# A streaming encoder layer on one core: the heads' mean squares and the samples' attention in column tiles of the array

## The chip, the cores and the metric

The kernel runs on one core of a Trainium2 chip. The metric is the device time of one execution in microseconds, from several runs of the same program; lower is better. The core has a matrix engine (PE, with its weight loads as PEld), a vector engine (DVE), a scalar engine (ACT), a general engine (POOL) and an engine that issues transfers (SP). Each takes its own instructions in a queue, and they wait for each other by semaphores.

## The reference

The reference is one layer of an encoder with two branches, for a prompt of 1024 frames and for 32 further frames of a running stream (here: the samples), which sees 512 cached frames. Width is 1024, all in fp32. One input projection gives the queries, keys and values of a gated linear attention (4 heads) and of a differential attention (8 heads of two 64-wide halves), and gates. What the change touches is the second branch:

```
def diff_attend(q, k, v, mask, lam):
    s = einsum('bqhmd,bkhmd->bhmqk', q, k) * (DIFF_HD ** -0.5)
    if mask is not None: s = where(mask, s, -inf)
    p = softmax(s, axis=-1)
    attn = p[:, :, 0] - lam * p[:, :, 1]
    return einsum('bhqk,bkhe->bqhe', attn, v)
...
yd = rmsnorm(o_diff, diff_subln_g) * (1 - lambda_init) * silu(dg)
merged = sigmoid(ma) * (yg @ w_proj_gla) + sigmoid(mb) * (yd @ w_proj_diff)
return x + rmsnorm(merged @ w_out, post_norm_g)
```

So each head has two score matrices, two softmaxes and one output of 128 channels for each frame, and that output is divided by the root of its mean square over the 128 channels.

## The kernel before

The work runs in stages: input norm and values (to about 270 us), the gated branch (to about 600 us), the differential branch (to about 1177 us), the projection of the gated branch (pg), the projection of the differential one (pd), and the output matrix with the last norm. Most matmuls run in a split form of three products (high times high, low times high, high times low), 352 or fewer columns each; these are the ps_w rows of lines 464 to 466, 486 to 488 and 1122 to 1124.

In the differential stage three threads share PE, and a planner (class `Order`, lines 62 to 123) writes out PE's order by hand while the program is built. A thread is a generator. It yields, ahead of a group of PE instructions, the group's cost in us, the events it needs with a latency each (table `W`, line 52), and the PSUM banks it takes; the planner keeps a clock, takes the first thread in its list that is ready, and adds the cost. The clock is the planner's own: nothing is measured. Only PE's order is fixed this way, the other engines' is left to the framework. The threads, first choice first:

- `diff_main` (line 923), the prompt's heads one after another. `diff_scores` (892) makes a 128-row tile of scores (ps_s, lines 906 and 907) and its softmax on DVE and ACT; the tile is transposed (ps_t, 954) and multiplied with the values (po, 967 to 969). Output `osb` and its square `sqo` (970, 971) hold a head transposed, channels on the 128 partitions and 1024 frames along them. `diff_fin` (878) then forms the mean square of each frame, which is a sum over partitions and so a matmul with `one_h`, a 128x128 matrix of 1/128: two steps of 512 frames into a bank `o` (ps_m, 882). All 128 result rows are equal; ACT copies row 0 back into `sqo` (883), and SP stores the 1024 numbers as row h of `msd` (885). Then DVE multiplies `osb` by the gate (888) and SP stores it (889). The steps of head h run just behind the first score tile of head h + 1. `sqo` has one buffer. `msd` is read once, behind the stage (1154), for all heads' roots; the roots come back as `rsb` and scale the loaded `ydr` (1164).
- `sample_thread` (977), the 32 samples, two heads at a time. Their keys are loaded from the cache (`load_k`), then the scores come: head and half m lie in rows ((h - h0) * 2 + m) * 32 of one bank, so four tiles of 64 rows x 32 columns of the array are used (ps_ss, lines 1009 and 1011, at `tile_position=(m * HD, r0)`; 512 cached and 32 own keys). Each head is a step of its own, with its value load (`load_v`) issued behind it on SP; the values take the place of the keys in SBUF. Softmax, transposes (ps_st, 1029), and the outputs: each head is a step that takes the bank `o`, four 128-row matmuls over the cached values and one 32-row matmul over the own ones, all in one strip of 32 columns (po_s, 1041 and 1042), and one ACT copy (1043). Norm and a transpose (ps_so, 1052) end the pair.
- `fill` (469), projections of the input for later heads and for the gates, in pieces of two k-steps (ps_w, 486 to 488). It runs where the others are not ready. The stage ends when the last head's output and the last of these jobs are done.

In this stage there are two banks for ps_w (`pj`), two double ones for scores (`s`), one for transposes (`t`) and one for outputs (`o`). An fp32 matmul that is not split is run by PE as two passes, each with its own weight load.

Of the kernel before, what the change touches and what calls it, by code (L numbers as in the profile page):

```python
# [14 lines left out]
AF = mybir.ActivationFunctionType  # L15
# [5 lines left out]
P = 128  # L21
NP = 1024
NS = 32
# [3 lines left out]
PAST = 512  # L27
GH, GDV = 4, 256
DH, HD = 8, 64
# [97 lines left out]
def hybrid_step_kernel(ctx: ExitStack, tc: tile.TileContext, a):  # L127
    nc = tc.nc
    mm = nc.tensor.matmul
    act = nc.scalar.activation  # L130
    ve = nc.vector
    dma = nc.sync.dma_start
    st = nc.sync.dma_start
# [26 lines left out]
    def dbank(name):  # L160
        return bank_of("s", name)
# [4 lines left out]
    def obank(name):  # L166
        return bank_of("o", name)
# [16 lines left out]
    one_h = cst.tile([P, P], F32, name="one_h")  # L184
# [691 lines left out]
        return BLK_DG + h, ("dg", h), begin, [(("fin", h - 1), 0.0)] if h else []  # L876

    def diff_fin(h, osb, sqo):
        for n0 in (0, 512):
            yield 0.86, [(("pv", h, 3), W["pv"])], ["o"]  # L880
            ps = obank("ps_m")
            mm(ps, one_h, sqo[:, n0 : n0 + 512], start=True, stop=True)
            act(sqo[0:1, n0 : n0 + 512], ps[0:1], AF.Copy)
            S.free("o", W["m_o"])
        st(msd[h : h + 1, :], sqo[0:1, :])
# [91 lines left out]
    def sample_thread():  # L977
# [11 lines left out]
        def load_v(h):  # L989
            vcs = ctile(h, [P, 4, P], "vcs")  # L990
            dma(vcs, a["cachev"][:, h * P : h * P + P].rearrange("(c p) e -> p c e", p=P))
            dma(vsm[0:NS, h % 2], a["newv"][NP:T, h * P : h * P + P])
            S.mark(("sv", h))
            return vcs

        for h0 in range(0, DH, 2):
            hs = (h0, h0 + 1)
            kcs = [load_k(h) for h in hs]
            vcs = []
            for h, kc in zip(hs, kcs):  # L1000
                if h == h0:
                    yield 0.6, [(("dk", h0 + 1), W["sdk"]), (("dg", h0 + 1), W["sdg"]), (("kc", h), W["kc"])], ["s"]
                    ps = dbank("ps_ss")
                else:
                    yield 0.6, [(("kc", h), W["kc"])], []
                for m in range(2):
                    r0 = ((h - h0) * 2 + m) * 32
                    hr = slice(m * HD, m * HD + HD)
                    mm(ps[r0 : r0 + 32, 0:PAST], qsam[h][hr, :], kc[hr, :], start=True, stop=True,
                       tile_position=(m * HD, r0))  # L1010
                    mm(ps[r0 : r0 + 32, PAST:w], qsam[h][hr, :], ksam[h][hr, :], start=True, stop=True,
                       tile_position=(m * HD, r0))
# [20 lines left out]
                S.free("t", W["st_t"])  # L1033
            S.mark(("spt", h0))
            os_ = tp.tile([64, P], F32, tag="yt", name="os_")
            for h in hs:
                yield 0.6, [(("spt", h0), W["spt"]), (("sv", h), W["sv"])], ["o"]
                r = slice((h - h0) * 32, (h - h0) * 32 + 32)
                o = obank("po_s")[r, 0:P]
                for c in range(4):  # L1040
                    mm(o, pT[:, c, h - h0, :], vcs[h - h0][:, c, :], start=(c == 0), stop=False, tile_position=(0, r.start))
                mm(o, pT[0:NS, 4, h - h0, :], vsm[0:NS, h - h0], start=False, stop=True, tile_position=(0, r.start))
                act(os_[r], o, AF.Copy)
# [281 lines left out]
```

## Time and profile before

| | us |
|---|---|
| median of 3 runs | 1478.51 |
| lowest, highest | 1473.87, 1479.91 |
| the profiled execution | 1477.82 |
| its span, first to last instruction | 1476.1 |
| mean granted clock of PE | 0.99 |
| ps_m, po_s, ps_ss groups (PE busy, 600 to 1177 us) | 14.4, 11.7, 6.7 |
| PE busy in that stage's ps_w (L486 to L488) | 754.2 |

The page gives, for each engine, busy time and its share of the span. Matmuls overlap each other in PE, so their printed durations add up to more than the time they fill (the last row of the table is longer than the stage); the distance from one start to the next is what a matmul takes of PE. A row of the timeline holds start, duration, engine, line, operation, what is written from what, the part of the array as rows*columns, the shape, and the count of merged instructions. A row of the chain of waits says who waited for whom: us in total, times, longest us.

### The profile page before, as it was taken

To read this page: it belongs to the slowest core of one execution; us is meant where nothing else is said; L and a number is where in the kernel's file an instruction comes from. 1 tells how busy PE (TensorE), PEld (TensorE's weight loads), DVE (VectorE), ACT (ScalarE), POOL (GpSimd) and SP (SyncE) were. 2 spreads that over 40 slices of the span, in tenths; PEclk is the share of its full clock that TensorE was granted. 3 is DMA by queue.
4 is the path that set the end of the run, shared out by engine and by line. 5 is a ranking of instruction groups with operands and counts; after the bars stand their busy time and mean duration, and the time that the engine had idled before them with its cause. 6 is when DMAs were issued, how large, how long until landed. Compare 5 with 4: busy or idle time off the path is not lost.

```text
span 1476.1 us, 22367 instructions
## 1 busy us (share of the span) xinstructions
PE 1422.4 (96%) x8848; PEld 1327.5 (90%) x8848; DVE 789.9 (54%) x1464; ACT 600.5 (41%) x1262; POOL 300.2 (20%) x186
## 2 busy tenths in 40 slices
PE   8999999989999999899999999999899899999997
PEld 6787779889999899899989998998899799999997
DVE  5602005756565343576776766678665536455415
ACT  4513114535354233455555555555455432221311
POOL 1200002222223124223222222222221111122001
PEclk9999999999999999999999999999999999999999
DMA  8620111122222233313232332223222278634205
GB/s 303 211 107 31 45 50 50 54 73 73 87 64 86 71 109 110 98 54 116 68 100 69 97 90 93 75 77 90 92 69 80 96 265 306 222 132 132 101 1 193
DMA packets 66742, 156.58 MB, mean 106 GB/s; under 512 B 10008, under 2 KB 28568, under 8 KB 65600
## 3 DMA queue, kind: packets, MB, share of 16 engines
q1 hardware_dynamic: 66624, 155.01, 32.5%
q8 instruction: 74, 1.21, 0.4%
q14 instruction: 44, 0.36, 0.1%
HBM read 104.39 MB, written 40.04 MB: 98 GB/s over the span
## 4 chain that ended last, share of the span: by engine, by line
PE 51%; DVE 6%; DMA 4%; ACT 2%; issue 1%; POOL 1%; SPq 0%; DVEq 0%; POOLq 0%; ACTq 0%
PE ps_w L486 9%; PE ps_w L487 9%; PE ps_w L488 9%; PE ps_w L465 2%; PE ps_w L464 2%; PE ps_w L466 2%; PE ps_s L907 2%; PE ps_t L954 2%; PE ps_s L906 2%; PE ps_c L1216 2%; PE ps_c L1218 2%; PE ps_c L1217 2%; DMA ydr<-ydd 1%; DMA kl<-kl 1%; PE po L968 1%
## 5 line engine op out<-in xcount | busy, mean ns | idle before, releaser
L486 PE MATMUL ps_w<-X,wh 128*128 128x352 f32 x1344 | 452.5, 337 | 1.4 <-DVE vo L292 1.1
L487 PE MATMUL ps_w<-X,wl 128*128 128x352 f32 x1344 | 437.7, 326 | 0.0
L488 PE MATMUL ps_w<-X,wh 128*128 128x352 f32 x1344 | 435.7, 324 | 0.0
L456 POOL TENSOR_TENSOR wl<-wr,wh 128x1024 fp32r<-128x1024 f32 x72 | 180.5, 2507 | 656.3 <-ACT wh L454 493.1
L486 PEld LDWEIGHTS ps_w<-X,wh 128*128 128x128 f32 x1344 | 255.0, 190 | 5.5 <-issue 3.0
L487 PEld LDWEIGHTS ps_w<-X,wl 128*128 128x128 f32 x1344 | 255.4, 190 | 1.2 <-issue 1.2
L488 PEld LDWEIGHTS ps_w<-X,wh 128*128 128x128 f32 x1344 | 254.7, 190 | 0.0
L912 ACT ACTIVATE p<-ps_s,nm 128x256 f32<-128x256 f32 (+7 forms) x128 | 94.6, 741 | 58.8 <-DVE ps_s L908 30.8
L306 PE MATMUL ps_v<-wh,X 128*128 128x512 f32 x248 | 97.6, 394 | 1.2 <-DVE X L245 1.2
L305 PE MATMUL ps_v<-wh,X 128*128 128x512 f32 x248 | 98.5, 397 | 0.2 <-DVE g L343 0.2
L307 PE MATMUL ps_v<-wl,X 128*128 128x512 f32 x248 | 98.3, 396 | 0.0
L454 ACT ACTIVATE wh<-wr 128x1024 fp32r<-128x1024 f32 x72 | 75.9, 1054 | 54.6 <-PE ps_w L488 30.6
L910 DVE TENSOR_REDUCE nm<-ps_s 128x1 f32<-128x256 f32 (+7 forms) x128 | 94.8, 747 | 2.7
L292 DVE TENSOR_TENSOR vo<-ps_v,vo 32x512 f32<-32x512 f32 x4 | 2.7, 678 | 140.8 <-ACT vo L291 140.8
L908 DVE MEMSET ps_s<- 64x64 f32 x128 | 14.3, 112 | 115.9 <-PE ps_s L907 114.3
L671 POOL TENSOR_TENSOR vl<-vr,vh 128x512 fp32r<-128x512 f32 (+1 forms) x20 | 24.6, 1228 | 219.4 <-ACT vh L670 219.4
L906 PE MATMUL ps_s<-k,q 128*128 128x512 f32 (+2 forms) x192 | 68.0, 362 | 1.2 <-DMA k<-k 1.2
L907 PE MATMUL ps_s<-kl,q 128*128 128x512 f32 (+2 forms) x192 | 63.8, 348 | 3.7 <-DMA kl<-kl 3.7
L288 ACT ACTIVATE vo<-ps_v 128x512 f32<-128x512 f32 x32 | 19.1, 595 | 115.1 <-PE ps_v L307 114.7
L956 ACT ACTIVATE ah<-ps_t 128x512 fp32r<-128x512 f32 (+2 forms) x96 | 46.9, 488 | 43.5 <-PE ps_t L954 42.7
L957 DVE TENSOR_TENSOR al<-ps_t,ah 128x512 fp32r<-128x512 f32 (+2 forms) x96 | 53.2, 554 | 18.3 <-ACT ah L956 17.0
L465 PE MATMUL ps_w<-Y,wl 128*128 128x352 f32 x192 | 62.2, 324 | 0.0
(319 smaller groups left out, 2968.8 us busy)
## 6 DMA issues: line engine op xcount, KB each, us to landing
wr<-w SPq DMA_DIRECT2D x72, 512.0 KB
thd<-gate SPq DMA_DIRECT2D x16, 528.0 KB
xn<-xn SPq DMA_DIRECT2D x16, 512.0 KB
wr<-wv SPq DMA_DIRECT2D x16, 512.0 KB
newk<-rr SPq DMA_DIRECT2D x8, 528.0 KB
ygr<-ygd SPq DMA_DIRECT2D x8, 528.0 KB
tha<-thd SPq DMA_DIRECT2D x8, 528.0 KB
ydr<-ydd SPq DMA_DIRECT2D x8, 528.0 KB
```

The lines of the kernel that those rows point to most:

```text
L305: mm(ps, xk[:, 0, t0 : t0 + P], wh[:, k, :], start=(k == 0), stop=False)
L306: mm(ps, xk[:, 1, t0 : t0 + P], wh[:, k, :], start=False, stop=False)
L307: mm(ps, xk[:, 0, t0 : t0 + P], wl[:, k, :], start=False, stop=(k == KT - 1))
L456: nc.gpsimd.tensor_tensor(wl, wr, wh.bitcast(F32), op=ALU.subtract)
L465: mm(ps[:, :n], wl[:, k, :], src[k][:, 0, t0 : t0 + n], start=False, stop=False)
L486: mm(ps[:, :n], wh[:, k, :], src[k][:, 0, t0 : t0 + n], start=(k == 0), stop=False)
L487: mm(ps[:, :n], wl[:, k, :], src[k][:, 0, t0 : t0 + n], start=False, stop=False)
L488: mm(ps[:, :n], wh[:, k, :], src[k][:, 1, t0 : t0 + n], start=False, stop=(k == KT - 1))
L906: mm(ps[:, n0 : n0 + n], qs[m][:, qsl], ks[m][:, n0 : n0 + n], start=True, stop=False)
L907: mm(ps[:, n0 : n0 + n], qs[m][:, qsl], kls[m][:, n0 : n0 + n], start=False, stop=True)
L910: ve.tensor_reduce(nm, ps[:, 0:w], axis=AX.X, op=ALU.max, negate=True)
L912: act(p[:, 0:w], ps[:, 0:w], AF.Exp, bias=nm, accum_out=sm[:, m : m + 1])
```

## The change

Three edits. `diff_fin` has one step in place of two. The 1024 frames of `sqo` are taken as four runs of 256, each multiplied with 32 columns of `one_h` into its own 32 partitions of one bank, at column positions 0, 32, 64 and 96 of the array; ACT copies the 128x256 block back, and the store takes one row out of each 32 as a quarter of `msd[h]`. The step's cost in the plan is 0.5 (it was 0.86 twice).

```
-        for n0 in (0, 512):
-            yield 0.86, [(("pv", h, 3), W["pv"])], ["o"]
-            ps = obank("ps_m")
-            mm(ps, one_h, sqo[:, n0 : n0 + 512], start=True, stop=True)
-            act(sqo[0:1, n0 : n0 + 512], ps[0:1], AF.Copy)
-            S.free("o", W["m_o"])
-        st(msd[h : h + 1, :], sqo[0:1, :])
+        yield 0.5, [(("pv", h, 3), W["pv"])], ["o"]
+        ps = obank("ps_m")[:, 0:256]
+        for n in range(4):
+            mm(ps[32 * n : 32 * n + 32], one_h[:, 0:32], sqo[:, n * 256 : n * 256 + 256], start=True, stop=True,
+               tile_position=(0, 32 * n))
+        act(sqo[:, 0:256], ps, AF.Copy)
+        S.free("o", W["m_o"])
+        st(msd[h].rearrange("(n t) -> n t", n=4), sqo[0:P:32, 0:256])
```

The samples' scores of both heads of a pair are one step (cost 1.1, was 0.6 twice), which needs both heads' cached keys; first the four matmuls over cached keys, then the four over own keys, and the value loads of both heads behind them.

```
-            vcs = []
-            for h, kc in zip(hs, kcs):
-                if h == h0:
-                    yield 0.6, [(("dk", h0 + 1), W["sdk"]), (("dg", h0 + 1), W["sdg"]), (("kc", h), W["kc"])], ["s"]
-                    ps = dbank("ps_ss")
-                else:
-                    yield 0.6, [(("kc", h), W["kc"])], []
-                for m in range(2):
...
-                vcs.append(load_v(h))
+            yield 1.1, [(("dk", h0 + 1), W["sdk"]), (("dg", h0 + 1), W["sdg"])] + [(("kc", h), W["kc"]) for h in hs], ["s"]
+            ps = dbank("ps_ss")
+            for cached in (True, False):
+                for h, kc in zip(hs, kcs):
+                    for m in range(2):
+                        r0 = ((h - h0) * 2 + m) * 32
+                        hr = slice(m * HD, m * HD + HD)
+                        k, c = (kc, slice(0, PAST)) if cached else (ksam[h], slice(PAST, w))
+                        mm(ps[r0 : r0 + 32, c], qsam[h][hr, :], k[hr, :], start=True, stop=True,
+                           tile_position=(m * HD, r0))
+            vcs = [load_v(h) for h in hs]
```

The samples' outputs of both heads are one step (cost 0.8, was 0.6 twice), which needs both heads' values; the heads alternate, head n in the strip of columns 32n, and one ACT copy takes both.

```
-            for h in hs:
-                yield 0.6, [(("spt", h0), W["spt"]), (("sv", h), W["sv"])], ["o"]
...
-                act(os_[r], o, AF.Copy)
-                S.free("o", W["so_o"])
+            yield 0.8, [(("spt", h0), W["spt"])] + [(("sv", h), W["sv"]) for h in hs], ["o"]
+            o = obank("po_s")[:, 0:P]
+            for c in range(5):
+                for n in range(2):
+                    kw, v = (P, vcs[n][:, c, :]) if c < 4 else (NS, vsm[0:NS, n])
+                    mm(o[32 * n : 32 * n + 32], pT[0:kw, c, n, :], v, start=(c == 0), stop=(c == 4),
+                       tile_position=(0, 32 * n))
+            act(os_, o[0:64], AF.Copy)
+            S.free("o", W["so_o"])
```

More of the change, by code (lines that the diff above doesn't have):

```diff
@@ L998, in sample_thread @@
             kcs = [load_k(h) for h in hs]
-            vcs = []
-            for h, kc in zip(hs, kcs):
-                if h == h0:
-                    yield 0.6, [(("dk", h0 + 1), W["sdk"]), (("dg", h0 + 1), W["sdg"]), (("kc", h), W["kc"])], ["s"]
-                    ps = dbank("ps_ss")
-                else:
-                    yield 0.6, [(("kc", h), W["kc"])], []
-                for m in range(2):
[L1007 to L1012, printed above, removed]
-                vcs.append(load_v(h))
+            yield 1.1, [(("dk", h0 + 1), W["sdk"]), (("dg", h0 + 1), W["sdg"])] + [(("kc", h), W["kc"]) for h in hs], ["s"]
[9 more added lines that the diff above has]
+            vcs = [load_v(h) for h in hs]
             nm = tp.tile([P, 1], F32, tag="nm", name="nm")
@@ L1035, in sample_thread @@
             os_ = tp.tile([64, P], F32, tag="yt", name="os_")
-            for h in hs:
-                yield 0.6, [(("spt", h0), W["spt"]), (("sv", h), W["sv"])], ["o"]
[L1038 to L1043, printed above, removed]
-                S.free("o", W["so_o"])
+            yield 0.8, [(("spt", h0), W["spt"])] + [(("sv", h), W["sv"]) for h in hs], ["o"]
[7 more added lines that the diff above has]
+            S.free("o", W["so_o"])
             ss = tp.tile([64, 1], F32, tag="ss", name="ss")
```

## The prediction

> **What bounds the kernel now.** I read the page's engine line first, then the busy time by stretches and the list of who waited for whom, then the timeline of PE around each operation that the diff touches, and the chain of waits for the places where PE is not the one that is late.
>
> ```profile
> PE 1422.4 (96%) x8848; PEld 1327.5 (90%) x8848; DVE 789.9 (54%) x1464; ACT 600.5 (41%) x1262; POOL 300.2 (20%) x186
> ```
>
> PE is busy for 96% of the span. A share over the whole span says nothing of one stage, so here are three stretches, two inside the differential-attention stage (about 600 to 1177 us, where all of the edits lie) and one just behind it:
>
> ```profile
> core 0: us, PE busy (x) PEld busy (x) DVE busy (x) ACT busy (x) POOL busy (x), PEclk, DMA share, GB/s
> 700.00:800.00 100.00, 96.79 (x628) 90.32 (x627) 69.66 (x135) 51.89 (x119) 23.37 (x11) 1.00 0.27 77
> ...
> 1000.00:1100.00 100.00, 93.97 (x601) 87.76 (x600) 72.57 (x135) 51.11 (x120) 24.37 (x12) 0.98 0.27 80
> ...
> 1200.00:1260.00 60.00, 59.39 (x366) 58.51 (x366) 29.81 (x31) 17.68 (x16) 14.48 (x6) 1.00 0.83 301
> ```
>
> In both stretches of the stage PE is busy 94 to 97 us of 100, at a full clock, while DVE has 27 us free and ACT 48. What PE waits for, from 600 to 1177 us:
>
> ```profile
> PE ps_t L954 <- DVE al L957: 4.1, 3, 1.4
> PE ps_st L1029 <- DVE smp L1032: 3.6, 2, 2.3
> PE ps_t L954 <- DVE smp L1055: 1.7, 1, 1.7
> PE ps_so L1052 <- DVE al L957: 1.2, 2, 0.7
> PE ps_s L907 <- DMA kl<-kl: 1.0, 2, 0.5
> PE ps_t L954 <- DVE ps_s L908: 0.9, 3, 0.3
> PE po L967 <- ACT os__13014 L1043: 0.4, 1, 0.4
> PE ps_t L954 <- DVE p L917: 0.3, 1, 0.3
> ```
>
> Together 13.2 us of 577. The planner puts a projection matmul (ps_w) into nearly every gap, so a slot of PE that is freed is taken by the next step. In this stage a microsecond less on PE is a microsecond less in the stage, up to where the projections run out. So I price the edits in PE slots: from the start of one matmul to the start of the next, since the printed durations overlap.
>
> **Heads' mean squares (L880 to L885).** Before, each head has two steps, each one 128x512 fp32 matmul that runs as two passes:
>
> ```profile
> 671.73 0.32 PE L488 MATMUL ps_w<-X,wh 128*128 128x352 f32 x1
> 671.89 1.02 PE L882 MATMUL ps_m<-sqo,one_h 128*128 128x512 f32 x2
> 672.35 0.73 PE L486 MATMUL ps_w<-X,wh 128*128 128x352 f32 x1
> 672.92 0.32 PE L487 MATMUL ps_w<-X,wl 128*128 128x352 f32 x1
> ```
>
> A ps_w slot is 0.16 us (671.73 to 671.89). From 671.89 to 672.92 is 1.03; less one ps_w slot, the pair takes 0.87 us, 0.435 a pass of 512 columns. How often:
>
> ```profile
> L882 PE MATMUL ps_m<-sqo,one_h 128*128 128x512 f32 x28 | 14.4, 595 | 0.0
> L1041 PE MATMUL po_s<-vcs,smp 128*32 128x128 f32 x64 | 8.5, 276 | 0.0
> ```
>
> 28 passes up to 1177 us are the 14 matmuls of heads 0 to 6: 14 x 0.87 = 12.2 us. (Head 7's two come later.)
>
> After, a head has one step of four matmuls of 256 columns, each in its own strip of 32 columns of the array. The trace holds this kind of work in the samples' scores, which already use four tiles (64 rows x 32 columns):
>
> ```profile
> 730.02 0.32 PE L488 MATMUL ps_w<-X,wh 128*128 128x352 f32 x1
> 730.26 1.08 PE L1009 MATMUL ps_ss<-kc,smp 64*32 64x512 f32 x8
> 731.15 0.26 PE L1011 MATMUL ps_ss<-smp 64*32 64x32 f32 x8
> 731.34 0.43 PE L486 MATMUL ps_w<-X,wh 128*128 128x352 f32 x1
> 731.60 0.32 PE L487 MATMUL ps_w<-X,wl 128*128 128x352 f32 x1
> ```
>
> Eight passes of 512 columns take 0.89 us (730.26 to 731.15); one after another they would take 8 x 0.435 = 3.5. So four run at a time, two rounds. The timeline cut at 730.35 us shows the first round alone, four passes begun within 0.09 us:
>
> ```profile
> 730.26 0.65 PE L1009 MATMUL ps_ss<-kc,smp 64*32 64x512 f32 x4
> ```
>
> The same rows price the change to tiles and back. In: 730.02 to 730.26, less the 0.16 slot, 0.08. Out: L486 to L487 is 0.26 in place of 0.16, 0.10. And 731.15 to 731.34 is 0.19 for two rounds of 32 columns, which by the pass above are 0.03 each: 0.13 of stagger and draining. A new step is thus 2 rounds x 0.435/2 + 0.13 + 0.18 = 0.74 us, and seven take 5.2: **7.0 us saved**. What no row shows is four streams through all 128 rows; in the scores each half of the rows carries two. Bounds: four at once 0.74, two at once 1.18, none at once 2.05. I take 0.74, since the one row with four tiles shows four.
>
> On ACT one copy of 128x256 replaces two of 1x512; ACT has 48 us free in 100 and no row of the waits above names this copy, so nothing. If it did name it, the bank would still come back once a head and not twice, which is a gain. The store of the result now has four rows of 1 KB where it had one of 4 KB; its issue was:
>
> ```profile
> L885 SPq DMA_DIRECT2D msd<-sqo x8: 235/245/253, 676.4 to 1189.6; - x8
> ```
>
> SP waits in order, and what is queued behind this store are the weight loads; they wait for the copy once, as before. Between nothing and one such issue more a head, 8 x 0.25 = 2 us, all on SP; PE's list above shows no wait for a weight load, so I take nothing. Head 7's step falls into the projection stage, where PE waits for its data anyway (last fence of this part): between 0 and 1.0 us, I take 0.
>
> **Samples' outputs (L1036 to L1044).** Before, each head has its own step: 8 passes of 128 columns (64 in all = 8 heads) and two on 32 rows:
>
> ```profile
> 748.16 1.06 PE L1041 MATMUL po_s<-vcs,smp 128*32 128x128 f32 x8
> 749.15 0.40 PE L1042 MATMUL po_s<-smp 32*32 32x128 f32 x2
> 749.48 0.43 PE L486 MATMUL ps_w<-X,wh 128*128 128x352 f32 x1
> ```
>
> 1.32 us inside, and 0.18 into tiles and out: 1.50 us, 8 times, 12.0 us. These passes use one strip of 32 columns and follow each other at 1.32/10. After, the two heads of a pair alternate in two strips. If strips run beside each other as in the scores, the pair's step is as long as one head's: 4 x 1.50 = 6.0, **6.0 us saved**. The bounds are that and no overlap, 4 x (2 x 1.32 + 0.18) = 11.3, 0.7 saved. I take the first. For the last pair the second step lay on the chain itself, with the bank's copy behind it:
>
> ```profile
> 1172.57 1.06 PE L1041 MATMUL po_s<-vcs,smp 128*32 128x128 f32 x8
> ...
> 1174.32 0.39 PE L967 MATMUL po<-ah,vh 128*128 128x256 f32 x1 [0.36 <-ACT os__13014 L1043]
> ...
> 1186.67 0.43 PE L1124 MATMUL ps_w<-y,wh 128*128 128x352 f32 x1 [0.51 <-DVE y L1093]
> ```
>
> So there the saving holds although the projections have run out: 1.75 us from 1172.57 to 1174.32 go. (The last row is PE waiting for data around head 7's mean square.) The merged step waits for both heads' value loads and for the bank at once; behind it on PE stand the ps_w and ps_s matmuls. No row of the waits names a value load, so I price this at nothing.
>
> **Samples' scores (L1000 to L1013).** The order inside a tile stays cached keys, then own keys; only the order between tiles changes. At 730 us the planner had already put both heads next to each other, and all 16 passes took 1.07 us. A gain is left only where it had not, and of the four pairs that is one; its second head came by itself, four passes of 512 columns and not eight:
>
> ```profile
> 877.27 1.06 PE L1009 MATMUL ps_ss<-kc,smp 64*32 64x512 f32 x4
> 878.15 0.23 PE L1011 MATMUL ps_ss<-smp 64*32 64x32 f32 x4
> 878.32 0.43 PE L486 MATMUL ps_w<-X,wh 128*128 128x352 f32 x1
> ```
>
> The second half's 1.05 us and its 0.18 of changes go: **1.2 us saved**. The value loads, which were issued between the heads, now come behind both; that is at most 1.1 us later on SP, and the values are used at 748.16, 17 us behind the scores. Hidden by that stretch; without it 4 x 1.1 us.
>
> **Sum.** 7.0 + 6.0 + 1.2 = 14.2 us. The profiled execution took 1477.82 us around a span of 1476.1, 0.7 below the median of the runs. 1477.8 - 14.2 = 1463.6 us.
>
> **Rivals.** (a) PE starts matmuls strictly in their order. Then a mean square's second pass, queued behind its first in the same strip, holds up the next strip: five rounds in place of two, 3 x 0.218 = 0.65 us a head, and in the outputs 11 rounds for 10, 0.1 a pair. The saving is 14.2 - 7 x 0.65 - 0.4 = 9.2 us, 1468.6. In the code the own keys of each tile stand ahead of the next tile's cached keys, yet all eight L1009 passes began ahead of the first L1011; that speaks against it, if PE's queue has the code's order. The Trainium skill (TensorE: Matmul & The Clock Gate, Part 3, what overlaps and what doesn't) does say that matmuls start and end in program order; by that rule the time would be the 1468.6 of this rival, and the trace does not bear the rule out. The rival has 7%. Its neighbour, two strips at a time, saves 7 x 0.44 = 3.1 us less, 1466.7; 7%.
>
> (b) Strips of full height do not overlap at all: mean squares 7 x (2.05 - 1.74) = 2.2 us longer, outputs 0.7 and scores 1.2 shorter: 1478.1. The scores' row speaks against it. 3%.
>
> (c) The gain is lost behind the stage. There PE is 99% busy but the DMA engines are too, with 83% (1200 to 1260), and they bring the next projection its ydr (L1089). These loads stand behind head 7's own steps and so move with them; but if the queues move less than PE does, half of the gain goes, 1470.7. 10%, half of it on either side of that.
>
> (d) The changed costs move every step of the plan, and the 13.2 us of waits are drawn anew. A few us either way lie in the forecast; 4 to 8 us more give 1468 to 1472. 12%.
>
> (e) Slower: less PE work between heads lets PE reach a head's first scores before its keys' copies have landed:
>
> ```profile
> 1102.32 6.11 DMA kl<-kl
> ```
>
> Now that costs 1.0 us in all. If seven heads waited 2.0 us each, the gain would be gone; at 3.1 us each, 21.7 in all, it is 7.5 us slower, and at the whole 6.1 it would be 1506. Against it: the planner's clock now charges 0.5 and 0.8 us for steps that I put at 0.74 and 1.50, so it allows the copies more real time, not less. 5%.
>
> **Numbers.** My forecast, 1463.6 give or take the waits, has 56%. 0.5% of the time is 7.4 us, about what a measurement of this kernel can tell from no change; faster means below 1471. The forecast, (a) with its neighbour, three quarters of (d) and half of (c) lie there: 56 + 14 + 9 + 5, 0.84. Same are (b) and the rest of (c) and (d): 0.11. Slower is (e): 0.05. The range runs from 1458, where head 7's 1.0 us and some 4.5 us of waits go too, to 1471, which takes in (a) and most of (d) and leaves out 16 in 100 above.
>
> **What would show it.** Right: four L882-like matmuls of 128*32, 128x256, starting within 0.1 us of each other, their slot near 0.74; po_s in four groups of 1.3 us; one group of 16 score passes in every pair; the last po matmul about 14 us earlier than 1177, and the last instruction by the same. Wrong: the four strips in a staircase (a); rows of PE waiting for kl or smp that add up to over 20 us in the stage (d, e); the stage 14 us shorter but the end not (c).

## The result, and the profile after

| us | before | after |
|---|---|---|
| median | 1477.95 (6 runs, 1473.87 to 1480.96) | 1487.78 (6 runs, 1486.10 to 1491.33) |
| profiled execution, its span | 1477.82, 1476.1 | 1490.72, 1488.9 |
| mean granted clock of PE | 0.99 | 0.982 |

The ratio is 1.0073, with a 95% interval of 1.0057 to 1.0088: slower, by 9.8 us. The forecast was 1463.6 us, so it misses by 24.2 us, and in the sign.

The engine line of the page after:

```profile
PE 1415.8 (95%) x8880; PEld 1325.6 (89%) x8880; DVE 807.0 (54%) x1464; ACT 591.1 (40%) x1250; POOL 299.8 (20%) x186
```

PE has less work (1422.4 before) in a span that is 12.8 us longer. So the instructions did not become dearer; PE stands idle, or runs slow. The groups themselves, from PE's timeline after: the heads' mean squares, the samples' outputs, and the samples' scores.

```profile
670.75 0.32 PE L488 MATMUL ps_w<-X,wh 128*128 128x352 f32 x1
671.00 0.64 PE L883 MATMUL ps_m<-sqo,one_h 128*32 128x256 f32 x8
671.57 0.43 PE L486 MATMUL ps_w<-X,wh 128*128 128x352 f32 x1
671.83 0.32 PE L487 MATMUL ps_w<-X,wl 128*128 128x352 f32 x1
...
728.56 1.06 PE L1010 MATMUL ps_ss<-kc,smp 64*32 64x512 f32 x8
729.44 0.24 PE L1010 MATMUL ps_ss<-smp 64*32 64x32 f32 x8
729.61 0.43 PE L486 MATMUL ps_w<-X,wh 128*128 128x352 f32 x1
...
746.55 1.07 PE L1041 MATMUL po_s<-vcs,smp 128*32 128x128 f32 x16
747.54 0.41 PE L1041 MATMUL po_s<-smp 32*32 32x128 f32 x4
747.88 0.38 PE L908 MATMUL ps_s<-k,q 128*128 128x256 f32 x1
```

Eight passes of a mean square take 0.57 us (671.00 to 671.57), plus 0.09 in (670.75 to 671.00, less a slot of 0.16) and 0.10 out: 0.76 us, where 0.74 was forecast. Sixteen score passes of both heads take 1.05 us, and the twenty output passes of both heads 1.33 us, as long as one head's before. Cut at 671.05 us, the timeline shows the four strips at once:

```profile
671.00 0.42 PE L883 MATMUL ps_m<-sqo,one_h 128*32 128x256 f32 x4
```

The stretches that answer to those of before:

```profile
700.00:800.00 100.00, 96.10 (x646) 91.13 (x645) 74.49 (x139) 51.82 (x118) 24.37 (x11) 1.00 0.26 74
...
1000.00:1100.00 100.00, 94.55 (x623) 88.84 (x622) 75.25 (x141) 51.66 (x123) 24.23 (x11) 0.98 0.29 82
...
1160.00:1200.00 40.00, 30.16 (x170) 25.78 (x169) 17.71 (x25) 15.00 (x26) 2.97 (x2) 0.79 0.46 156
1200.00:1260.00 60.00, 54.21 (x324) 53.34 (x323) 24.81 (x26) 16.59 (x15) 11.40 (x5) 0.97 0.76 260
```

By busy share the middle of the stage looks as before. What differs by it is the end, where PE has 30.16 us of 40 at a clock of 0.79 (before: 35.27 at 0.96), and the next stage (54.21 of 60, before 59.39). What PE waits for from 600 us to the stage's last matmul at 1183.9:

```profile
PE ps_st L1028 <- DVE smp L1031: 8.7, 4, 2.6
PE ps_t L956 <- DVE al L959: 8.6, 8, 1.6
PE ps_t L956 <- DVE ps_s L910: 5.8, 4, 2.5
PE ps_st L1028 <- DVE al L959: 2.1, 1, 2.1
PE ps_so L1052 <- DVE al L959: 1.4, 1, 1.4
```

26.6 us, against 13.2 before. None of it is for a transfer of keys; all of it is for DVE, by a transpose (ps_t, ps_st, ps_so) whose bank or operand DVE has not finished. One such place, PE first, then DVE and POOL in the same 4 us:

```profile
741.17 0.64 PE L883 MATMUL ps_m<-sqo,one_h 128*32 128x256 f32 x8
744.42 0.27 PE L1028 MATMUL ps_st<-ident,p 128*32 128x128 f32 x1 [2.61 <-DVE smp L1031]
```

```profile
740.43 2.37 POOL L938 TENSOR_TENSOR vl<-vr,vh 128x1024 fp32r<-128x1024 f32 x1 [9.79 <-ACT vh L937]
740.93 2.95 DVE L890 SCALAR_TENSOR_TENSOR osb<-osb,gs_half,sg 128x1024 f32<-128x1024 f32 x1 [0.38 <-ACT osb L973]
743.80 0.15 DVE L917 RECIPROCAL sm<-sm 128x2 f32<-128x2 f32 x1
743.88 0.40 DVE L1031 TENSOR_TENSOR smp<-ps_st,smp 128x256 f32<-128x256 f32 x1
```

PE's next instruction behind the mean square is the samples' last transpose, whose bank is freed by DVE's add (L1031, 743.88). On DVE that add stands behind the gate multiply of the head (L890), which takes 2.95 us. PE had no projection piece in between. It came so in heads 1, 3 and 5. Before, the same wait (ps_st, smp) made 3.6 us in two places.

To add all this up, PE's timeline of each kernel was cut into parts: the stage from its first score matmul to its last projection matmul (L486 to L488), in that part every gap above 0.45 us beyond the matmul's own slot ("waits"), half of the time at half clock ("clock"), and the rest ("work"); then the tail to the last po matmul; then the time from there to the first matmul of the pd stage. From pd to the end it is 196.1 us in both. (A gap is the distance from one start to the next, less the slot. The first 12 us of the stage are left in the work: there PE waits 3.3 us for `kl` in every one of the kernels below, and its clock is at half for 6.8 us, in e18 for 3.4.)

| us | start of the stage | work | waits | clock | tail | to pd | span |
|---|---|---|---|---|---|---|---|
| before | 595.7 | 557.5 | 13.2 | 1.7 | 8.9 | 102.9 | 1476.1 |
| after | 595.2 | 544.2 | 22.0 | 5.1 | 17.3 | 108.9 | 1488.9 |

The work fell by 13.3 us, nearly what was forecast. It was given back twice over, in four places: waits 8.8, clock 3.4, tail 8.4, next stage 6.0.

The tail, in the timeline of PE and in stretches of 4 us:

```profile
1166.55 0.32 PE L488 MATMUL ps_w<-X,wh 128*128 128x352 f32 x1
1166.71 0.49 PE L956 MATMUL ps_t<-ident,p 128*128 128x128 f32 x3
1169.34 0.66 PE L1028 MATMUL ps_st<-ident,p 128*128 128x128 f32 x4 [2.15 <-DVE al L959]
...
1176.30 1.11 PE L956 MATMUL ps_t<-ident,p 128*128 128x128 f32 x4 [1.50 <-DVE al L959]
...
1179.50 0.41 PE L970 MATMUL po<-al,vh 128*128 128x256 f32 x1
1179.71 0.41 PE L971 MATMUL po<-ah,vl 128*128 128x256 f32 x1
```

```profile
1172.00:1176.00 4.00, 2.79 (x20) 1.54 (x16) 0.78 (x3) 1.27 (x4) 0.54 (x1) 0.50 0.36 123
1176.00:1180.00 4.00, 2.29 (x9) 1.77 (x10) 1.34 (x4) 0.60 (x1) 0.00 (x0) 0.50 0.00 0
1180.00:1184.00 4.00, 4.00 (x22) 4.00 (x21) 0.00 (x0) 0.00 (x0) 0.00 (x0) 0.55 0.66 206
```

The projections run out at 1166.55 while the last head's transposes, a whole pair of samples' transposes and outputs and the last po are still to come. Before, the samples' transposes began at 1166.85, while projections still ran (to 1168.10), and half of the outputs came right behind. After, each wait is bare, and behind the waits PE is granted half its clock: four transposes take 0.66 us at 1169.34 and 1.11 at 1176.30. In the built order, 343 of the 380 projection pieces (six matmuls each) that lie behind the stage's first score matmul stand ahead of the mean square of head 6; before, it was 340. So three pieces fewer were left for the end.

In the next stage PE waits for the gated branch's evacuation (`tha`, the step that takes the sums out of PSUM) on DVE, from 1184 us on after and from 1177 us on before:

```profile
PE ps_w L486 <- DVE tha L1105: 5.7, 4, 2.7
```

```profile
PE ps_w L486 <- DVE tha L1105: 0.8, 2, 0.5
```

That evacuation stands behind DVE's scaling of ydr (L1164). After, DVE sits idle in front of that scaling for 13.7 us, waiting for the loads of ydr and rsb, before for 6.0.

### The profile page after: what moved, and what is told of

It is laid out like the page before. It is cut to its first block, busy times and chain, and to the rows that moved or that the text cites. A ratio compares the mean times of both kernels' runs of the same rounds, so it can differ in the third digit from the quotient of the medians.

```text
span 1488.9 us, 22417 instructions
## 1 busy us (share of the span) xinstructions
PE 1415.8 (95%) x8880; PEld 1325.6 (89%) x8880; DVE 807.0 (54%) x1464; ACT 591.1 (40%) x1250; POOL 299.8 (20%) x186
## 4 chain that ended last, share of the span: by engine, by line
PE 46%; DVE 11%; ACT 4%; DMA 3%; issue 2%; POOL 1%; SPq 0%; DVEq 0%; POOLq 0%; ACTq 0%
PE ps_w L486 8%; PE ps_w L487 8%; PE ps_w L488 8%; PE ps_w L465 2%; PE ps_w L464 2%; PE ps_w L466 2%; PE ps_s L908 2%; PE ps_s L909 2%; PE ps_t L956 2%; PE ps_c L1216 2%; PE ps_c L1218 2%; PE ps_c L1217 2%; ACT p L914 1%; DVE p L919 1%; PE po L970 1%
## 5 line engine op out<-in xcount | busy, mean ns | idle before, releaser
L486 PE MATMUL ps_w<-X,wh 128*128 128x352 f32 x1344 | 451.3, 336 | 1.4 <-DVE vo L292 1.1
L488 PE MATMUL ps_w<-X,wh 128*128 128x352 f32 x1344 | 436.4, 325 | 0.0
L486 PEld LDWEIGHTS ps_w<-X,wh 128*128 128x128 f32 x1344 | 255.8, 190 | 4.8 <-issue 2.5
L488 PEld LDWEIGHTS ps_w<-X,wh 128*128 128x128 f32 x1344 | 255.3, 190 | 0.0
L919 DVE SCALAR_TENSOR_TENSOR p<-p,sm 128x128 f32<-128x128 f32 (+3 forms) x64 | 67.1, 1048 | 1.7
```

Source lines behind the costliest of these rows:

```text
L486: mm(ps[:, :n], wh[:, k, :], src[k][:, 0, t0 : t0 + n], start=(k == 0), stop=False)
L488: mm(ps[:, :n], wh[:, k, :], src[k][:, 1, t0 : t0 + n], start=False, stop=(k == KT - 1))
L919: ve.scalar_tensor_tensor(pt[0][:, 0:w], pt[0][:, 0:w], sm[:, 0:1], pt[1][:, 0:w], op0=ALU.mult, op1=ALU.add)
```

## The experiments

The theory formed from this: the instructions are as cheap as priced, but the planner, given new costs (0.5, 1.1, 0.8), wrote another order of PE for the whole stage, in which more transposes reach PE before DVE is done with them. The rivals: one of the three groups brings the waits itself; DVE is made slow by POOL or by its gate multiply, whatever the order; the planner's latencies are too short. All ratios are to the kernel before, on the same chip. Four groups of runs had medians of 1476.83, 1478.60, 1477.25 and 1477.47 us of it, the last two runs 1477.78.

### The new instructions in the old order, and each part alone

Run e1: the three new groups, but every old step and cost of the plan is kept, with the second (or first) step of a pair empty.

```
+        for n0 in (0, 512):
+            yield 0.86, [(("pv", h, 3), W["pv"])], ["o"]
+            if n0 == 0:
...
+            S.free("o", W["m_o"])
```

> Theory 1 (the order): the tiled groups take the PE time that was forecast, and the loss comes from the new order that the planner makes of the changed costs. With the new groups in exactly the order of before the kernel is faster by 10 to 15 us. Theory 2 (less PE work): the stage cannot use the PE time that is freed, because the vector engine's chain sets its pace; then this kernel is no faster than before, and PE's waits grow by as much as the groups shrink. Theory 3 (the tiles): changing the array's division hurts the matmuls around it or the clock; then it is as slow as the change, plus 8 to 10 us.

Measured: 1468.87 us, ratio 0.9937 (0.9919 to 0.9955), 8.0 us faster. Outside the three groups, the built order of PE is that of before, instruction by instruction. By the same cut of the timeline the work is 545.0, the waits 14.7, the clock 1.7, the tail 11.3, to pd 102.9. The work is 12.5 us less than before, and 1.5 of waits and 2.4 of tail are given back. The gain is short of the 10 to 15 us of theory 1, but theory 2 (no gain) and theory 3 (a loss of 8 to 10 us) both fall. So the instructions gain; it is their order in the change that loses.

Run e2: the heads' mean squares alone, with the cost 0.5 of the change.

> The mean squares alone, with a new order. Theory 1: the part's 7 us less work and a newly drawn order, anywhere from -12 to +12 us, and the three edits alone do not add up to the whole. Theory 3, with the fault in the mean squares (three of the long waits stand right behind them): slower by 8 to 14 us.

Measured: 1497.50 us, ratio 1.0130 (1.0093 to 1.0166), 20.7 us slower: a miss, outside the ranges of both theories. What a new order can cost was put too low here too.

Run e3: the samples' outputs alone, cost 0.8.

> The samples' outputs alone, with a new order. Theory 1: 6 us less work and a newly drawn order, -11 to +11 us. Theory 3, with the fault in the mean squares: faster by 5 to 6 us.

Measured: 1472.52 us, ratio 0.9972 (0.9956 to 0.9988), 4.3 faster. That lies in the wide range of theory 1, and near the 5 to 6 of theory 3, so it decides nothing between them.

Run e4: the samples' scores alone, cost 1.1; PE's order comes out as before but for the passes inside the step.

> The samples' scores alone, which takes 1.2 us off PE in one pair and changes no other pair's work. Theory 1: if it moves by more than 3 us either way, that is the order and nothing else. Theories 2 and 3: within 2 us of before.

Measured: 1477.72 us, ratio 1.0000 (0.9983 to 1.0017). With the order unchanged all three theories allow this; a saving of 1.2 us is too small to be told from none here.

The parts add up to 20.7 - 4.3 + 0.9 = 17.3 us slower, the whole is 9.8 slower: they are not additive, as parts that only shift each other's order need not be. The part with the largest saving (mean squares, 7.0 us of slots) is the one that loses.

### The costs without the instructions

Run e6: the kernel before, one number changed.

```
-            yield 0.86, [(("pv", h, 3), W["pv"])], ["o"]
+            yield 0.25, [(("pv", h, 3), W["pv"])], ["o"]
```

> The kernel before with one number changed: the plan charges 0.25 for each of the two steps of a mean square in place of 0.86. Every instruction of the program is one of before, PE's work is the same, only the order can differ. Theory 1 (the order): slower by 10 us or more, as the edit of the mean squares alone was, plus the 7 us that it saved. Theory 2 (less PE work) and theory 3 (the tiles): within 3 us of before.

Measured: 1510.13 us, ratio 1.0215 (1.0180 to 1.0251), 31.5 us slower with not one instruction changed. What PE waits for from 600 to 1190 us in it:

```profile
PE ps_t L954 <- DVE ps_s L908: 13.3, 5, 3.4
PE ps_st L1029 <- DVE smp L1032: 6.9, 3, 2.3
PE ps_t L954 <- DVE al L957: 6.6, 6, 1.6
```

These are the three largest rows of after again, 26.8 us together against 23.1: the first is larger here (13.3 for 5.8), the other two a little smaller. 0.61 us less charged for a step is enough to bring them about.

### The plan told what the steps take

Run e5: the change, with its three costs set to what the steps take on PE.

```
-        yield 0.5, [(("pv", h, 3), W["pv"])], ["o"]
+        yield 0.74, [(("pv", h, 3), W["pv"])], ["o"]
```

In the same way 1.1 became 1.25 for the scores and 0.8 became 1.5 for the outputs.

> The change, with the plan charging what the three groups really took of PE (0.74, 1.25 and 1.50 us in place of 0.5, 1.1 and 0.8). If the fault is that the changed costs are too low, the time comes back to 1470 us or less. If a plan's order is as good as a drawn lot, whatever its costs, it lies anywhere from 1470 to 1510.

Measured: 1464.19 us, ratio 0.9906 (0.9888 to 0.9923), 13.1 us faster than before and 23.6 faster than the change. PE's three largest waits in it from 600 to 1190 us that lie in the stage:

```profile
PE ps_s L909 <- DMA kl<-kl: 4.3, 4, 2.2
PE ps_t L956 <- DVE al L959: 3.3, 1, 3.3
PE ps_st L1028 <- DVE smp L1031: 2.7, 2, 1.4
```

The place of 741 us, in the timeline of PE in e5:

```profile
742.59 0.64 PE L883 MATMUL ps_m<-sqo,one_h 128*32 128x256 f32 x8
743.16 0.43 PE L486 MATMUL ps_w<-X,wh 128*128 128x352 f32 x1
...
744.07 0.33 PE L488 MATMUL ps_w<-X,wh 128*128 128x352 f32 x1
744.28 0.28 PE L1028 MATMUL ps_st<-ident,p 128*32 128x128 f32 x1
```

One piece of six projection matmuls now stands between the two, and the wait is gone. By the cut of the timeline:

| us | start | work | waits | clock | tail | to pd | span |
|---|---|---|---|---|---|---|---|
| after | 595.2 | 544.2 | 22.0 | 5.1 | 17.3 | 108.9 | 1488.9 |
| e1 | 595.3 | 545.0 | 14.7 | 1.7 | 11.3 | 102.9 | 1467.1 |
| e5 | 597.9 | 543.4 | 5.9 | 0.0 | 12.7 | 108.9 | 1464.9 |
| e18 (below) | 599.0 | 545.0 | 10.9 | 0.0 | 2.8 | 110.0 | 1463.7 |

The work is the same within 2 us in all four. Of the 24.0 us of span between after and e5, 16.1 are waits, 5.1 clock and 4.6 tail; the later start takes back 2.7. The 6.0 us of the next stage are lost in e5 too. By the same cut they go with the outputs planned as one step: to pd it is 107.1 us in e3 (outputs alone), but 102.5 in e2 (mean squares alone) and 102.9 in e4 (scores alone).

### Is it that the costs are honest?

If honest costs were the reason, costs above the truth should lose, and the kernel before should gain from honest costs.

Run e15, the change with 0.80, 1.30 and 1.60 in the places of e5:

> The change with costs a little over the measured ones (0.80, 1.3, 1.6). PE's order differs from that of the measured costs only in one transpose that stands six matmuls later, at four places. If the number of pieces decides: within 3 us of the measured costs' 1464. If an order is a drawn lot that any exchange draws anew: 5 us or more away.

Measured: 1465.16 us, ratio 0.9914 (0.9879 to 0.9948), within 1 us of e5. So not every exchange in the order draws the time anew.

Run e18, with 1.1, 1.9 and 2.2, half as much again as the steps take:

> The change with costs half again over the measured ones (1.1, 1.9, 2.2). Pieces ahead of heads 2, 4 and 6: 389, 435 and 482. If fewer pieces ahead are better throughout: 1464 us or less. If there is a best number near that of the measured costs: slower than 1470.

Measured: 1464.95 us, ratio 0.9903 (0.9865 to 0.9940): no worse. Its waits lie elsewhere. In the stage those for `kl` lead, the tail is nearly gone, and the longest single wait is that for `y` at the start of the next stage:

```profile
PE ps_w L1122 <- ACT y L1092: 7.7, 1, 7.7
PE ps_s L909 <- DMA kl<-kl: 6.6, 8, 2.2
```

Run e17, the kernel before with honest costs (0.87; 0.63 for a head's scores; 1.50 in place of 0.6 for a head's outputs), no instruction changed:

> The kernel before, its instructions untouched, with the plan charging what they took of PE (0.87, 0.63 and 1.50 us in place of 0.86, 0.6 and 0.6). Up to head 6 the same number of pieces stands ahead of each head as before, and at the last head four pieces fewer (501 for 505), which then remain for its end. If the number of pieces decides: 2 to 6 us faster than before. If the lot decides: anywhere within 15 us.

Measured: 1491.42 us, ratio 1.0097 (1.0068 to 1.0126), 14.0 us slower. The cut gives work 555.4, waits 18.7, clock 8.6, tail 3.2, to pd 111.2. A miss: honest costs are not better in themselves, and the sign for the same kind of correction turns over between two kernels.

Run e19, the change with 0.5 for the mean squares of heads 0 to 3 and 0.74 behind them:

```
-        yield 0.5, [(("pv", h, 3), W["pv"])], ["o"]
+        yield 0.5 if h < 4 else 0.74, [(("pv", h, 3), W["pv"])], ["o"]
```

> The change with the mean square's cost at 0.5 for heads 0 to 3 and at 0.74 for heads 4 to 7; the other costs as in the change. Two of the change's three extra pieces stay. If each extra piece costs its share: two thirds of the way from 1464 to 1488, 1475 to 1484. If the last one alone (the end without projections) costs it: 1470 or less.

Measured: 1488.45 us, ratio 1.0078 (1.0056 to 1.0100): as slow as the change, where a place between was expected. The 2.98 us from the start of a mean square's last pass to that of the transpose are there again in heads 1, 3 and also 5, though head 5's own step is charged in full. The low charge of the first heads shifts the pieces, and the shift stays.

### DVE, POOL and the latencies

Run e8, the kernel before without POOL's part of splitting the stage's projection weights into high and low:

```
+        if psum["banks"] is BANKS and b < BLK_PG:
+            return wh, wh
```

> The kernel before, where the projections of the differential stage take the weights' high part also for the second product: the general engine's split of the weights (2.4 us each, 32 of them) is left out, PE's work and the plan stay. Theory 1a (the vector engine's operations are drawn out where they meet a split on the general engine, and that makes the bank late): the vector engine's busy time in the stage falls by 20 us or more and PE's waits to under half; the time falls by 3 to 8 us. Theory 1b (the bank is late because the vector engine's own queue is in a worse order): within 2 us of before.

Measured: 1472.49 us, ratio 0.9958 (0.9943 to 0.9973), 6.1 us faster. The time is that of theory 1a, but its reasons are seen in part only: DVE's busy time from 600 to 1166 us falls by 7.1 us (391.4 to 384.2) and not by 20, and PE's waits by the cut fall from 13.2 to 10.0 and not to half.

Run e9, the same in the change:

> The same with the change. Theory 1a: PE's waits fall far more than in the kernel before, the time falls by 15 us or more from the change's, and the change is then faster than the kernel before by its 14 us, give or take 4. Theory 1b: still slower than the kernel before with the same part left out.

Measured: 1479.07 us, ratio 1.0011 (0.9993 to 1.0030). POOL's work costs the change 8.7 us and the kernel before 6.1. The difference between the two kernels is still 6.6 us of 9.8, as theory 1b has it. DVE's operations next to POOL's are a part of the loss, and not what makes the change slower.

Run e10, the change with the gate multiply of heads 0 to 6 taken from DVE to POOL and ACT; PE's order is that of the change.

```
-            ve.scalar_tensor_tensor(osb[:, c], osb[:, c], gs_half, dsg[h][:, c], op0=ALU.mult, op1=ALU.mult)
+            nc.gpsimd.tensor_tensor(osb[:, c], osb[:, c], dsg[h][:, c], op=ALU.mult)
+            act(osb[:, c], osb[:, c], AF.Copy, scale=gs_half)
```

> The change with PE's order as it is; for heads 0 to 6 the multiplication of a head's output by its gate (2.95 us on the vector engine, behind which PE stands for 2.98 us three times) is done by the general engine and the scalar engine. Theory 1b (PE's hand-written order meets a vector engine that is in the middle of something else): the three waits go and the time falls by 6 to 11 us from the change's. If the waits only move to the next operation in the vector engine's queue: within 3 us of the change.

Measured: 1495.14 us, ratio 1.0119 (1.0092 to 1.0147), 7.4 us slower than the change: a miss, since neither outcome allowed a loss. Two of its waits of PE:

```profile
PE po_s L1045 <- ACT sqo L885: 7.2, 3, 2.4
...
PE ps_st L1032 <- DVE smp L1035: 1.6, 4, 0.9
```

The wait behind the gate multiply went from 8.7 to 1.6 us, so the reading of 741 us was right for these waits. But ACT, now behind POOL's result, frees the bank `o` late, and DVE's softmax, with 16.7 us more of work on POOL, takes more time (the rows of `p`: 67.1 us in the change, 81.2 here):

```profile
L919 DVE SCALAR_TENSOR_TENSOR p<-p,sm 128x128 f32<-128x128 f32 (+3 forms) x64 | 67.1, 1048 | 1.7
L923 DVE SCALAR_TENSOR_TENSOR p<-p,sm 128x128 f32<-128x128 f32 (+3 forms) x64 | 81.2, 1268 | 1.7
```

Run e11, the same edit in e1:

> The changed groups in the order of before, with the gate's multiplication off the vector engine as well. In that order one such wait of 2.99 us is left. Theory 1b: 2 to 5 us faster than the order of before alone, so 10 to 14 us faster than the kernel before. If waits only move: within 2 us of it.

Measured: 1475.04 us, ratio 0.9982 (0.9970 to 0.9994), 6 us slower than e1. A miss. The softmax is drawn out here too (the rows of `p`: 56.5 us in e1, 70.7 here), and the waits of ps_t for DVE's `smp` (L1035 in e1, L1039 here) grow from 0.7 to 5.0 us. A wait for ACT's copy of the mean square is not among them.

Run e7, the change with longer latencies for the transposes' bank ("tr_t" 2.27 to 3.0, "st_t" 1.14 to 4.0):

> The change, with the plan holding the transposes' bank for 3.0 us (2.27) behind the prompt's transposes and 4.0 us (1.14) behind the samples'. In the traces the vector engine gives the bank back over 2.27 us behind the last transpose 39 times of 96 in the change, 28 of 96 before, and behind a sample's transposes 4.16 us in three of eight. Theory 1: the planner puts projections where PE stood, and the time falls by 8 us or more from the change's. Theories 2 and 3: within 4 us of the change.

Measured: 1507.92 us, ratio 1.0192 (1.0156 to 1.0229), slower. A miss: longer latencies everywhere move the whole order again, and not to a better one (waits 31.9, tail 24.9).

Run e12, the change with a gate's projections moved towards the end, so that the tail has cover:

```
-GATES_DIFF = [2, 1, 1, 1, 1, 1, 1, 2, 2]
+GATES_DIFF = [2, 1, 1, 1, 0, 1, 1, 2, 3]
```

> The change, with one of the gates' projections (24 slots of 0.16 us in each of three pieces, 11.6 us) moved from the seventh head's share to the last one's, which also draws a new order. Theory 2b (the last head's chain runs without projections beside it, 17.3 us in the change, 8.9 before): that stretch falls to 10 us or less. The time falls by the same 7 us if the rest of the order is no worse; if it rises, the sum of PE's waits ahead of that stretch says by how much the lot was worse.

Measured: 1491.13 us, ratio 1.0088 (1.0068 to 1.0109). The tail fell from 17.3 to 5.7 us as meant, but the order ahead of it was worse: the sum of waits is 31.8, and the largest row lies in the stretch of the fourth head, at 837 and 883 us. It is the fourth head that gave its pieces up (index 4 of the list), not the seventh, as the expectation has it:

```profile
PE ps_w L486 <- ACT rr L829: 11.0, 2, 6.0
```

### One place, in both directions

What was open: whether the 23.6 us between the change and e5 are single places, each worth its own wait, or one wait that breeds others. Run e20 is the change with one latency raised for three pairs, which moves exactly three pieces of six projection matmuls, in heads 1, 3 and 5, from behind the samples' last transpose to ahead of it. Run e21 is e5 with the reverse, by 0.0 in place of the 2.0 in this edit of e20.

```
-                S.free("t", W["st_t"])
+                S.free("t", 2.0 if h0 < 6 else W["st_t"])
```

> The change, with one latency of the plan raised for three of the four pairs of samples (the transposes' bank, 1.14 to 2.0). In the built order this moves exactly three projection pieces of six matmuls each (0.97 us a piece), those behind the mean squares of heads 1, 3 and 5, from behind the samples' last transpose to ahead of it; nothing else of PE's order changes. In the trace of the change PE stands there 2.6 us before that transpose, waiting for DVE. Theory L (each wait costs what PE lacks of work at that place, and no more): the three waits fall by 0.97 us each, 2.9 us in all, so 1484.9 us against 1487.8 of the change. Theory C (a late transpose delays the softmax, the copies and the next head's steps, so that a wait breeds others): 6 to 12 us less, 1476 to 1482, and the other waits of the stage fall too. Theory N (DVE's chain is what is full there, so the work moved in front is missed behind it): no gain, 1487 to 1489, with a wait of 1 us at the samples' outputs in its place.

Measured: 1485.52 us, ratio 1.0052 (1.0034 to 1.0069), 2.3 us less than the change (3.1 by the two ratios). Its row of that wait, 8.7 in the change:

```profile
PE ps_st L1028 <- DVE smp L1031: 5.3, 4, 1.5
```

> The reverse edit on the version with measured costs (0.74, 1.25, 1.50): the same latency lowered to 0 for three pairs, which moves exactly three pieces from ahead of the samples' last transpose to behind it, as the change has them. There the mean square's last round starts at 742.85 and DVE's operand is ready at 744.27, so PE would stand 1.1 us. Theory L: three waits of 1.0 to 1.1 us come, about 3 us more, 1467.3 against 1464.2. Theory C: 6 to 12 us more, 1470 to 1476, with waits spread over the stage. Theory N: no loss, 1463.5 to 1465. If L holds in both, the local place explains 6 us of the 23 between the two versions at most, and the remainder belongs to where the other pieces stand.

Measured: 1466.18 us, ratio 0.9931 (0.9910 to 0.9952), 2.0 us more than e5 (3.7 by the two ratios). Its row, 2.7 in e5:

```profile
PE ps_st L1028 <- DVE smp L1031: 6.0, 3, 2.5
```

The wait changed by 3.4 and 3.3 us, the time by 2.3 and 2.0. Each difference is near the noise of its pair (the intervals touch), but both lie near the 2.9 and 3 of theory L, that a wait costs itself. Of the 6 to 12 us of theory C, that it breeds others, the noise of a pair leaves only the lower end. Theory N, no gain, is not excluded by the times alone, but the wait at the samples' outputs that it asks for is not in e20's rows. So these three places hold 2 to 3 us for each piece moved in all of them, by estimate at most some 6 to 9 us if the whole of the three waits goes. The rows put the remainder of the 23.6 us in the other places (ps_t behind `al` and ps_s: 14.4 us after, 3.3 in e5), in the clock and in the tail.

## Why the prediction was wrong

**The prices were right.** Mean squares 0.76 us where 0.74 was forecast, outputs 1.33 inside where 1.32, one group of scores in every pair. The work of the stage is 13.3 us less after than before; 14.2 were forecast, with the last pair's 1.75 us in the tail and not in this count. Rival (a), matmuls that start strictly in order, and its neighbour fall: four passes start within 0.02 us of each other, the other four 0.24 us later, and the step takes the two rounds of 0.74 and not the five of rival (a). The rule of the Trainium skill that was weighed there (TensorE: Matmul & The Clock Gate, Part 3, what overlaps and what doesn't) does not hold for these tiles (the rows are in the last section). Rival (b), no overlap at full height, falls by the same rows.

**What failed is the step from PE's work to the stage's time: "In this stage a microsecond less on PE is a microsecond less in the stage".** It took the waits as they were, with 13.2 us, and after has 26.6 by the same view. The step can hold only for a fixed order in which PE is the one that is late. Even in e1, whose order is the old one, 12.5 us of work gave 8.0 us of time. The change has not only shorter instructions but other numbers in the plan, and the plan wrote another order. The prediction saw this, as rival (d), "the 13.2 us of waits are drawn anew", and priced it at a few us either way, at worst 8, with 12 chances in 100. No row carried that price. The runs give the size: from numbers in the plan alone, with no instruction changed, the time moved by 31.5 us (e6), 14.0 us (e17) and 23.6 us (change to e5).

**The argument that the planner's clock "allows the copies more real time, not less" was wrong in effect.** It stood against rival (e), PE waiting for keys, and there it held: after has no such wait from 600 us on. But the charge that is too low for the mean squares let the plan put the samples' transposes right behind three of them, and the transposes wait for DVE, as those at other places do: 26.6 us of waits, all on DVE. The prediction looked at DVE's 27 us free in 100 and took it for slack. DVE is free on average and late at certain places, where a 2.95 us multiply or a softmax stands ahead of the one small operation that PE needs. (The wait for keys comes where PE is fastest, 4.3 us in e5 and 6.6 in e18, and costs less than it saves.)

**Tail and clock were costed at nothing.** The last pair's outputs are one group, as forecast, but at half clock it takes 2.42 us (1171.26 to 1173.68), so the 1.75 us were not gained in full. The tail grew by 8.4 us, since the pieces that had covered it were used up earlier, and PE at half clock then stretched the rest. Rival (c), a loss behind the stage, came true in part: the next stage lost 6.0 us, with the loads of ydr and rsb late, in e5 as well. The tail follows the pieces that the plan has left: with 343 of the 380 ahead of the mean square of head 6 it is 17.3 us (after); with 340 it is 8.9, 11.3 and 12.7 (before, e1, e5); with 337 and 335 it is 2.8 (e18) and 3.2 (e17).

**The forecast's figure** of 1463.6 us is what the change gives with costs to match, 1464.19 in e5. That is no proof of the forecast's sum: e5's gains and losses are others (waits 7.3 us less than before, next stage 6.0 more, and a start 2.2 later), so that the two figures meet is partly luck.

**What stays open.** That the order is the cause is shown by e1, e5 and e6. What makes one order better than another is shown only for single places (e20, e21, e10). That honest costs do it is refuted (e17, e18). Why the outputs planned as one step make the loads of the next stage late, where e1 with the same instructions in two steps does not, was not tried.

The version to keep is e5, 1464.19 us, with e15 and e18 equal to it within their intervals.

## What to carry to other kernels

In a kernel whose queue order is computed from a table of costs, a cost is part of the change: run the new instructions once in the old order and the old instructions once with the new costs, before judging either. A busy share of 96% says that shorter work can be worth its length, and only the list of waits of the new kernel, place by place, says whether its order let it be. Try several values of a cost around the measured one, and keep the one that measures best, since neither honest nor careful values are best by rule.

## What the runs showed of the hardware

- Four column strips of full height (128 rows x 32 columns) run beside each other: eight fp32 passes of 256 columns take 0.57 us, where one after another they would take 1.74 (an estimate, from 0.435 us a pass of 512 columns).
- Matmuls in different tiles of the array do not start in the order of the program. Before, the own keys of a tile stand ahead of the next tile's cached keys in PE's built order, yet all eight passes over cached keys (from 730.26 us) start ahead of the first over own keys (731.15). Of the four matmuls of a mean square, with two passes each, the timeline cut at 671.05 us holds four starts. The trace does not name the strips; that it is one start for each is the reading that fits the two rounds.
- Waits of some 2 us on PE were followed by half the granted clock: 0.50 from 1172 to 1180 us, with po matmuls 0.21 us apart (1179.50 to 1179.71), where before they were 0.12 apart (1174.78 to 1174.90). It is not a rule: of six waits of 2 to 3 us in after (at 741, 836, 889, 915, 1037 and 1167 us), four were followed by a stretch at half clock of 3.4 us or, in the tail, 13.7. So a short wait in the tail can cost more than itself.
- DVE's gate multiply takes 2.95 us while POOL runs its operation of 2.37 us (the rows at 740 us above), and 1.28 us for head 7, when POOL is idle. In the timeline of after:

```profile
1184.87 1.28 DVE L890 SCALAR_TENSOR_TENSOR osb<-osb,gs_half,sg 128x1024 f32<-128x1024 f32 x1 [5.24 <-ACT osb L973]
```

POOL's operation ends at 742.80 (740.43 and 2.37), DVE's at 743.88, 1.08 us later, close to the 1.28 it takes alone, so the multiply seems to have been held up for most of the 2.95 us and not slowed. The Trainium skill (SBUF — State Buffer, who interferes with whom) says that a DVE instruction with two inputs in SBUF contends with a POOL instruction that reads SBUF, and that the second to issue waits the other out; these rows agree, with half a microsecond between the two starts.
